# Low halves of split weights, kept in HBM and loaded again: one core of a hybrid recurrent decoder step

## The chip, the cores and the metric

One NeuronCore of a Trainium2 chip runs the kernel. It has five engines with instruction streams of their own, each in order: TensorE (PE; PEld is its weight load), VectorE (DVE), ScalarE (ACT), GpSimd (POOL) and SyncE (SP), which here issues every DMA. The metric is device time in microseconds (us) of one execution; the kernel before takes 3067.66 us (median of 3 runs, 3066.21 to 3068.48).

## The reference, cut to what matters

One layer of a decoder, for a prompt of 2048 tokens and 8 samples of 4 tokens, with 1024 channels, in fp32:

```python
h = layernorm(x)                                   # input layer norm, over 1024 channels
u = h @ w_in                                       # 1024 x 3860, columns for four groups of heads
y_a, y_b, y_c, y_d = delta(u_a), ssd(u_b), hgrn2(u_c), mlstm(u_d)   # chunkwise recurrences
mix = concat(y_a, y_b, y_c, y_d) @ w_out           # 1024 x 1024
h1 = layernorm(alpha * h + mix)
ff = square(relu(h1 @ w_up)) @ w_down              # 1024 x 4096, 4096 x 1024
out = layernorm(alpha * h1 + ff)
```

Outputs are `out` for prompt and samples, and the final states of the four recurrences.

## The kernel before, in words

The 2048 tokens are four blocks of 512 (`NB`, `TB`); the 32 sample tokens ride along with block 0 in the input projection and with block 2 afterwards, so those products are 544 wide. The order of stages is: input projection P of blocks 0 to 3, the output projection W of block 0 near the end of P 3, then for each block its feed-forward F, with W of the next block at F's end. The recurrences ("mixing", `gen_A` to `gen_D`) run in between, as chains of small operations on all engines, through P and most of F 0 to F 2.

**Products.** Weights come in *units* of 128 x 512 fp32 (256 KB): four 128x128 pieces of one column block. A product in fp32 accuracy is made of three passes in fp32r: a weight `w` is split into `hi = round(w)` and `lo = w - hi`, the data likewise, and PE adds `hi*xh + lo*xh + hi*xl`. In `gemm` each unit gives 12 matmuls (24 where the block is 544 wide). The list `units` (from `fill_units`) names all 832 units in order of use: 62 of w_in for each of four blocks, 16 of w_out for each, 64 of w_up for each, and 64 of w_dn for each, with the last 8 of them used twice in the last block.

**Supply of weights.** At each unit `cur`, `gemm` calls `w_pump`: it has SP load the raw units up to `cur + 4` (`w_get`, tile `wraw`), and splits the units up to `cur + 2` (`w_split`). A split is one operation that rounds (`whi`, on ACT mostly, line 253 like all operations of engines) and one subtraction (`wlo`, on POOL mostly, else on DVE). `wraw`, `whi` and `wlo` have four buffers each. A raw buffer comes free when its subtraction is done. Every block splits the same weights again. The first four units go another way, in `ln0_start`: `w_first` rounds, `w_rest` subtracts.

**What sets the order.** The program is written out by hand into one instruction stream for each engine while a planner (`_Run`) keeps an estimated clock for each engine. Each `tick` in `gemm` lets the mixing chains and the other streams go on that are ready by these clocks. `tvp` and `cpv` choose POOL or DVE, and ACT or DVE, by the same clocks. On the chip each engine follows its stream and waits on semaphores where its estimate was wrong. SP issues all DMAs in program order on one queue (line 374, `dma`); if one of them has to wait for its buffer or its data, those behind it wait too. The program gives SP's DMAs eight completion semaphores in turn, so a DMA also waits for the one eight places ahead of it.

**Input layer norm.** `ln0(b + 1)` runs beside P of block b: it normalizes, transposes, then stores the eight tiles of the block to `hTd` in HBM, which W reads again later, and splits six of them (`EARLY_P`).

Of the kernel before, what the change touches and what calls it, by code (L numbers as in the profile page):

```python
# [10 lines left out]
F32 = mybir.dt.float32  # L11
F32R = mybir.dt.float32r
# [10 lines left out]
TB = 512  # L23
# [15 lines left out]
EARLY_P = 6  # L39
# [4 lines left out]
LATE_W = 5.0  # L44
LATE_U = 3.0
LN1_PACE = 0.1
W0_AT = 29

# [297 lines left out]
def kernel(ctx: ExitStack, tc: tile.TileContext, t):  # L346
# [8 lines left out]
    sb4 = ctx.enter_context(tc.tile_pool(name="sb4", bufs=4))  # L355
    nbp = ctx.enter_context(tc.tile_pool(name="nbp", bufs=NBUF))
# [29 lines left out]
    def cp(out, in_, scale=1.0):  # L386
        A(out, in_, AF.Copy if scale == 1.0 else AF.Identity, scale)

    def tt(out, a, b, op, eng=None):
        (eng or V).tensor_tensor(out=out, in0=a, in1=b, op=op)  # L390
# [135 lines left out]

    def w_get(i):
        w = sb4.tile([128, 4, 128], F32, tag="wraw", name="wraw")
        dma(w, units[i])
        raws[i] = w  # L530

    def w_pump():
        cur = wst["cur"]
        while wst["nload"] < min(cur + 5, len(units)):
            i = wst["nload"]
            w_get(i)
            wst["nload"] += 1
            if wst["nsplit"] < min(cur + 3, wst["nload"]):
                w_split()
        while wst["nsplit"] < min(cur + 3, len(units)):  # L540
            w_split()

    def w_split():
        i = wst["nsplit"]
        w = raws.pop(i)
        hi = sb4.tile([128, 4, 128], F32R, tag="whi", name="whi")
        lo = sb4.tile([128, 4, 128], F32R, tag="wlo", name="wlo")
        cpv(hi, w, 512, LATE_W - 1.0)
        tt(lo, w, hi.bitcast(F32), sub, tvp(512, LATE_W))
        his[i] = (hi, lo)  # L550
        wst["nsplit"] += 1

    def w_first(i):
        hi = sb4.tile([128, 4, 128], F32R, tag="whi", name="whi")
        lo = sb4.tile([128, 4, 128], F32R, tag="wlo", name="wlo")
        cp(hi, raws[i])
        his[i] = (hi, lo)

    def w_rest(i, eng):
        hi, lo = his[i]  # L560
        tt(lo, raws.pop(i), hi.bitcast(F32), sub, eng)
# [109 lines left out]
    def ln0_start():  # L671
# [15 lines left out]
        w_get(3)  # L687
# [20 lines left out]
        w_rest(2, V)  # L708
        xs = xs[1:] + xs[:1]
# [20 lines left out]
        for k in range(8):  # L730
# [17 lines left out]
            if k == 5:  # L748
                for i in range(4, 8):
                    w_get(i)  # L750
                wst["nload"] = 8
# [12 lines left out]
    def ln0(b):  # L764
# [30 lines left out]
        yield from _stagger([one(i) for i in range(CPB)], 5)  # L795
        for k in range(8):
            dma(hTd[b][:, k, :], hT[b][k][:, 0:TB])
        queue_set(("P", b), hT[b], TB)
        for k in range(EARLY_P):
            yield  # L800
            split_next(("P", b))
# [1217 lines left out]
    def fill_units():  # L2019
        W = lambda: [units.extend([t["w_out_u"][d, 0], t["w_out_u"][d, 1]]) for d in range(8)]  # L2020
        for b in range(NB):
            for u in range(NPU):
                if b == NB - 1 and u == W0_AT:
                    W()
                units.extend([t["w_in_u"][u, 0], t["w_in_u"][u, 1]])
        for b in range(NB):
            f = 0
            for c in range(FFB):
                for j in range((4 if c == 0 else 3) + (1 if c + 1 < FFB else 0)):
                    units.extend([t["w_up_u"][f, 0], t["w_up_u"][f, 1]])  # L2030
                    f += 1
                if c == FFB - 1 and b + 1 < NB:
                    W()
                for q in range(2 if b == NB - 1 and c == FFB - 1 else 1):
                    units.extend(t["w_dn_u"][c, d] for d in range(8))
# [130 lines left out]
```

## Time and profile before

| | |
|---|---|
| median of 3 runs | 3067.66 us |
| the profiled execution, its time | 3071.5 us |
| its span, first to last instruction | 3069.7 us |
| PE busy | 2897.1 us, 94% |
| DVE, POOL, ACT busy | 2156.1, 1632.5, 1244.2 us |
| mean granted clock of PE | 0.983 |
| DMA | 407.10 MB, 133 GB/s; SP's queue takes 46.3% of the 16 DMA engines |

How to read it. Rows of groups give the line, engine and operation, then the tile written and the tiles read, the shape, how often, and behind the bar busy time in us and mean ns of one; behind the second bar the time in which the engine stood idle just before, and for whom. The tiles: `pd`, `pa`, `pb` are PSUM; `wraw`, `whi`, `wlo` the weights; `g` the 544-wide tiles of everything that isn't weights; `a`, `b`, `la..`, `kz..` those of the mixing chains; `U..`, `hTd`, `yTd` lie in HBM; `nb` is a tile broadcast from HBM (`ud32d`). Rows of waits give what an engine was about to run, for whom it waited, then the sum in us, the count and the longest. A matmul's end is modelled, so 100% busy says that PE had work, not that it ran at its peak.

### The profile page before, as it was taken

The page shows a single profiled execution, that of the slowest core. Times are in us where ns is not written, and L with a number is a line of the kernel's source. Part 1 is how long each engine was busy: PE and PEld are TensorE (multiplying, and loading weights), DVE is VectorE, ACT ScalarE, POOL GpSimd, SP SyncE. Part 2 cuts the span into 40 slices and gives each one's busy share as a digit, 9 for nine tenths or more (in the row PEclk, how much of TensorE's full clock was granted, in tenths as well). Part 3 has the DMA queues.
Part 4 walks back from the last instruction along what each step waited for, and adds up shares of the span by engine and source line. Part 5 has one row for each costly group of instructions (what it writes and reads, how often), then busy time and mean ns, then how long its engine had stood idle before and what let it go on. Part 6 is the DMA issues. An engine that isn't in the chain of part 4 may idle for free. (4 is left out here: it accounts for less than half of the span.)

```text
span 3069.7 us, 48033 instructions
## 1 busy us (share of the span) xinstructions
PE 2897.1 (94%) x16668; PEld 2479.8 (81%) x16668; DVE 2156.1 (70%) x4077; ACT 1244.2 (41%) x2653; POOL 1632.5 (53%) x1982
## 2 busy tenths in 40 slices
PE   7889899998999899999999999999999999999997
PEld 7778767777877778888787877778899999888886
DVE  6867887896986677777767865665887644474445
ACT  4554564564563533333244322233533222432222
POOL 5656664865664544554564536444363344444545
PEclk9999999999999999999999999999999999999998
DMA  6765465446556444454443435355343432333333
GB/s 188 85 186 166 121 190 164 130 129 201 121 159 192 139 120 124 132 173 119 138 145 115 144 91 139 118 159 153 92 147 105 125 93 84 112 120 93 99 95 98
DMA packets 361262, 407.10 MB, mean 133 GB/s; under 512 B 65468, under 2 KB 207804, under 8 KB 361020
## 3 DMA queue, kind: packets, MB, share of 16 engines
q1 hardware_dynamic: 361020, 404.04, 46.3%
q8 instruction: 132, 2.16, 0.3%
q14 instruction: 110, 0.90, 0.1%
HBM read 340.20 MB, written 63.72 MB: 132 GB/s over the span
## 5 line engine op out<-in xcount | busy, mean ns | idle before, releaser
L253 PE MATMUL pd<-g,whi 128*128 128x512 f32 (+2 forms) x8080 | 2242.6, 362 | 29.1 <-ACT g L253 17.2
L253 POOL TENSOR_TENSOR wlo<-wraw,whi 128x512 fp32r<-128x512 f32 x727 | 1031.8, 1426 | 1268.2 <-ACT whi L253 1071.8
L253 PEld LDWEIGHTS pd<-g,whi 128*128 128x128 f32 x8080 | 1393.6, 190 | 238.5 <-ACT g L253 19.4
L253 PE MATMUL pd<-g,wlo 128*128 128x512 f32 (+2 forms) x4040 | 1307.7, 355 | 16.4 <-POOL wlo L253 15.1
L253 PEld LDWEIGHTS pd<-g,wlo 128*128 128x128 f32 x4040 | 720.7, 190 | 113.2 <-POOL wlo L253 22.7
L253 ACT ACTIVATE whi<-wraw 128x512 fp32r<-128x512 f32 x797 | 489.2, 626 | 476.7 <-PE pd L253 256.0
L253 DVE TENSOR_TENSOR g<-g 128x512 fp32r<-128x512 f32 (+5 forms) x344 | 341.5, 995 | 157.2 <-ACT g L253 151.3
L253 ACT ACTIVATE g<-pd 128x512 f32<-128x512 f32 (+2 forms) x340 | 172.5, 526 | 473.7 <-PE pd L253 473.3
L253 DVE TENSOR_TENSOR g<-g,pd 128x512 f32<-128x512 f32 (+2 forms) x288 | 159.4, 570 | 211.7 <-PE pd L253 211.3
L253 ACT ACTIVATE g<-g 128x512 f32<-128x512 f32 (+4 forms) x350 | 212.9, 632 | 81.1 <-DVE g L253 40.1
L253 POOL TENSOR_TENSOR a<-nb,x 128x124 f32<-128x124 f32 (+30 forms) x496 | 198.4, 400 | 70.4 <-DMA nb<-ud32d 41.2
L253 POOL TENSOR_TENSOR x<-x,a 128x124 f32<-128x124 f32 (+30 forms) x496 | 199.5, 402 | 38.9
L253 DVE CAST g<-g 128x512 fp32r<-128x512 f32 (+1 forms) x162 | 158.4, 978 | 27.6 <-POOL g L253 21.2
L253 ACT ACTIVATE b<-b 128x256 f32<-128x256 f32 (+3 forms) x201 | 81.6, 406 | 182.2 <-DVE b L253 176.1
L253 DVE TENSOR_TENSOR wlo<-wraw,whi 128x512 fp32r<-128x512 f32 x105 | 83.1, 792 | 74.2 <-ACT whi L253 70.6
L253 DVE SCALAR_TENSOR_TENSOR g<-g 128x512 f32<-128x512 f32 (+3 forms) x124 | 117.8, 957 | 14.6 <-ACT g L253 14.2
L253 DVE SCALAR_TENSOR_TENSOR g<-g,par 128x512 f32<-128x512 f32 (+1 forms) x128 | 125.5, 998 | 0.1
L253 POOL TENSOR_TENSOR g<-g 128x512 f32<-128x512 f32 (+3 forms) x74 | 106.8, 1447 | 32.5 <-ACT g L253 25.1
L253 DVE TENSOR_TENSOR b<-laC 128x64 f32<-128x64 f32 (+3 forms) x466 | 110.2, 294 | 0.1
L253 DVE TENSOR_SCALAR g<-g 128x512 int32<-128x512 int32 (+6 forms) x137 | 79.7, 600 | 29.6 <-ACT g L253 28.7
L253 DVE TENSOR_TENSOR kzD<-laC,b 64x128 f32<-64x128 f32 (+1 forms) x228 | 98.6, 432 | 1.7
L253 DVE SCALAR_TENSOR_TENSOR g<-g,pd 128x512 f32<-128x512 f32 (+1 forms) x80 | 45.2, 581 | 67.0 <-PE pd L253 66.4
(2558 smaller groups left out, 2815.3 us busy)
## 6 DMA issues: line engine op xcount, KB each, us to landing
wraw<-in_w_dn_u_dram SPq DMA_DIRECT2D x264, 256.0 KB
wraw<-in_w_up_u_dram SPq DMA_DIRECT2D x256, 256.0 KB
wraw<-in_w_in_u_dram SPq DMA_DIRECT2D x248, 256.0 KB
nb<-ud32d SPq DMA_DIRECT2D x128, 256.0 KB
wraw<-in_w_out_u_dram SPq DMA_DIRECT2D x64, 256.0 KB
UC<-g SPq DMA_DIRECT2D x40, 256.0 KB
g<-in_x_prompt_dram SPq DMA_DIRECT2D x32, 256.0 KB
hTd<-g SPq DMA_DIRECT2D x32, 256.0 KB
```

The source lines that it names most:

```text
L253: r = f(*a, **k)
```

## The change

For each unit the program now counts its uses by name (`need`). A low half is subtracted at its first use, stored to HBM (`lod`) and from then on loaded beside the raw unit (`w_get`), straight into its buffer. For w_in the second making is the one stored (`KEEP`), so blocks 0 and 1 subtract and blocks 2 and 3 load. The store of unit i is issued when `cur` reaches i (`lo_keep`). `wraw` goes from four buffers to three, `wlo` from four to five. Of 832 low halves 268 are made, 206 stored and 564 loaded. In `ln0_start` the fourth unit is loaded after the first subtractions, and three units instead of four are loaded during the first transposes. In `ln0` the eight stores to `hTd` are issued one at each step of the stream, between the splits, and not in one go before them.

```diff
+KEEP = {"w_in_u": 2}
...
+    wrp = ctx.enter_context(tc.tile_pool(name="wrp", bufs=3))
+    wlp = ctx.enter_context(tc.tile_pool(name="wlp", bufs=5))
...
     def w_get(i):
-        w = sb4.tile([128, 4, 128], F32, tag="wraw", name="wraw")
+        w = wrp.tile([128, 4, 128], F32, tag="wraw", name="wraw")
         dma(w, units[i])
-        raws[i] = w
+        lo = None
+        if keys[i] in lod:
+            lo = wlp.tile([128, 4, 128], F32R, tag="wlo", name="wlo")
+            dma(lo.bitcast(F32), lod[keys[i]])
+        raws[i] = (w, lo)
+
+    def lo_make(i, hi, eng):
+
+        w, lo = raws.pop(i)
+        if lo is not None:
+            return lo
+        lo = wlp.tile([128, 4, 128], F32R, tag="wlo", name="wlo")
+        tt(lo, w, hi.bitcast(F32), sub, eng())
+        key = keys[i]
+        made[key] = made.get(key, 0) + 1
+        if made[key] == KEEP.get(key[0], 1) and uses[key] > made[key]:
+            kept.append((i, key, lo))
+        return lo
+
+    def lo_keep(n):
+        while kept and kept[0][0] <= n:
+            _, key, lo = kept.popleft()
+            lod[key] = drp.tile([128, 4, 128], F32, name=f"lod{len(lod)}")
+            dma(lod[key], lo.bitcast(F32))
 
     def w_pump():
         cur = wst["cur"]
+        lo_keep(cur)
         while wst["nload"] < min(cur + 5, len(units)):
...
     def w_split():
         i = wst["nsplit"]
-        w = raws.pop(i)
         hi = sb4.tile([128, 4, 128], F32R, tag="whi", name="whi")
-        lo = sb4.tile([128, 4, 128], F32R, tag="wlo", name="wlo")
-        cpv(hi, w, 512, LATE_W - 1.0)
-        tt(lo, w, hi.bitcast(F32), sub, tvp(512, LATE_W))
-        his[i] = (hi, lo)
+        cpv(hi, raws[i][0], 512, LATE_W - 1.0)
+        his[i] = (hi, lo_make(i, hi, lambda: tvp(512, LATE_W)))
         wst["nsplit"] += 1
...
         w_get(1)
-        w_get(3)
...
         w_rest(0, G)
         w_rest(2, V)
+        w_get(3)
...
             if k == 5:
-                for i in range(4, 8):
+                for i in range(4, 7):
                     w_get(i)
-                wst["nload"] = 8
+                wst["nload"] = 7
...
         yield from _stagger([one(i) for i in range(CPB)], 5)
+        queue_set(("P", b), hT[b], TB)
         for k in range(8):
             dma(hTd[b][:, k, :], hT[b][k][:, 0:TB])
-        queue_set(("P", b), hT[b], TB)
-        for k in range(EARLY_P):
-            yield
-            split_next(("P", b))
+            yield
+            if k < EARLY_P:
+                split_next(("P", b))
```

How the change moves instructions, at three places. First SP in P of block 2, around the stores of group A's gates (`UA`). In brackets stands what a DMA waits for: a compute engine, or one of the eight completion semaphores of earlier DMAs (`DMAHW`). Before:

```order
L374 DMA UA_169<-g 128x4x128 [waits DVE_49]
L374 DMA wraw<-in_w_in_u_dram 128x512 [waits DMAHW6_49,Pool_49]
L374 DMA wraw<-in_w_in_u_dram 128x512 [waits DMAHW7_49,Pool_49]
L374 DMA UA_169<-g 128x4x128 [waits DVE_49]
L374 DMA wraw<-in_w_in_u_dram 128x512 [waits DMAHW2_49,DMAHW0_49,Pool_49]
L374 DMA UA_169<-g 128x4x128 [waits DMAHW1_49,Pool_49]
```

After the change, at the same stores:

```order
L377 DMA UA_175<-g 128x4x128 [waits DVE_49]
L377 DMA UA_175<-g 128x4x128 [waits DMAHW0_49,DVE_49]
L377 DMA wraw<-in_w_in_u_dram 128x512 [waits DMAHW1_49,Activation_49]
L377 DMA wlo<-lod_4911 128x512 [waits DMAHW2_49,PE_49]
L377 DMA UA_175<-g 128x4x128 [waits DMAHW3_49,Pool_49]
L377 DMA UA_175<-g 128x4x128 [waits DMAHW4_49,DVE_49]
L377 DMA wraw<-in_w_in_u_dram 128x512 [waits DMAHW5_49,Activation_49]
L377 DMA wlo<-lod_4934 128x512 [waits DMAHW6_49,PE_49]
```

A raw load waited for POOL's subtraction; now it waits for the rounding on ACT, and a second load behind it waits for PE, whose matmuls free the `wlo` buffer.

Second, POOL at the first convolution of group A in P of block 2 (`a`, `x` are the scan of HGRN2, `halo` the convolution's border). Before:

```order
L253 TENSOR_TENSOR wlo<-wraw,whi 128x512
L253 COPY g<-haloA_119 128x3
L253 TENSOR_TENSOR wlo<-wraw,whi 128x512
L253 TENSOR_TENSOR a_5852<-nb,x_108 128x4x11
L253 TENSOR_TENSOR x_108<-x_108,a_5852 128x4x11
L253 TENSOR_TENSOR a_5852<-nb,x_108 128x4x10
```

After the change:

```order
L254 COPY g<-haloA_125 128x3
L254 TENSOR_TENSOR a_5984<-nb,x_114 128x4x11
L254 TENSOR_TENSOR x_114<-x_114,a_5984 128x4x11
L254 TENSOR_TENSOR a_5984<-nb,x_114 128x4x10
L254 TENSOR_TENSOR x_114<-x_114,a_5984 128x4x10
```

The subtractions are gone from POOL here. Over the whole program POOL's go from 727 to 224 and DVE's from 105 to 44; 20 operations of the last layer norm go from DVE to POOL.

Third, SP in P of block 1, at the input layer norm's stores of block 2. Before:

```order
L374 DMA wraw<-in_w_in_u_dram 128x512 x2
L374 DMA nb<-ud32d 128x1x512
L374 DMA hTd_152<-g 128x512 x8
L374 DMA wraw<-in_w_in_u_dram 128x512
L374 DMA UB_166<-g 128x4x128 x2
```

After the change:

```order
L377 DMA nb<-ud32d 128x1x512
L377 DMA hTd_158<-g 128x512
L377 DMA lod_5192<-wlo 128x512
L377 DMA wraw<-in_w_in_u_dram 128x512
L377 DMA UB_172<-g 128x4x128
L377 DMA lod_5229<-wlo 128x512
L377 DMA wraw<-in_w_in_u_dram 128x512
L377 DMA UB_172<-g 128x4x128
L377 DMA hTd_158<-g 128x512
```

The eight stores to `hTd` no longer stand in one row; between them stand the raw loads and, in this block, the stores of low halves.

More of the change, by code (lines that the diff above doesn't have):

```diff
@@ L525, with need @@
     raws, his = {}, {}
+    keys, uses, made, lod, kept = [], {}, {}, {}, deque()
+    def need(key, ap):
+        keys.append(key)
+        uses[key] = uses.get(key, 0) + 1
+        units.append(ap)
     def w_get(i):
-        w = sb4.tile([128, 4, 128], F32, tag="wraw", name="wraw")
+        w = wrp.tile([128, 4, 128], F32, tag="wraw", name="wraw")
         dma(w, units[i])
-        raws[i] = w
+        lo = None
[19 more added lines that the diff above has]
+            dma(lod[key], lo.bitcast(F32))
     def w_pump():
         cur = wst["cur"]
+        lo_keep(cur)
         while wst["nload"] < min(cur + 5, len(units)):
-            i = wst["nload"]
-            w_get(i)
+            w_get(wst["nload"])
             wst["nload"] += 1
@@ L554, in w_first @@
         hi = sb4.tile([128, 4, 128], F32R, tag="whi", name="whi")
-        lo = sb4.tile([128, 4, 128], F32R, tag="wlo", name="wlo")
-        cp(hi, raws[i])
-        his[i] = (hi, lo)
+        cp(hi, raws[i][0])
+        his[i] = (hi, None)
     def w_rest(i, eng):
-        hi, lo = his[i]
-        tt(lo, raws.pop(i), hi.bitcast(F32), sub, eng)
+        hi, _ = his[i]
+        his[i] = (hi, lo_make(i, hi, lambda: eng))
     def pieces(nt):
@@ L2019, in fill_units, with half @@
     def fill_units():
-        W = lambda: [units.extend([t["w_out_u"][d, 0], t["w_out_u"][d, 1]]) for d in range(8)]
+        def half(name, u):
+            for k in range(2):
+                need((name, u, k), t[name][u, k])
+        W = lambda: [half("w_out_u", d) for d in range(8)]
         for b in range(NB):
@@ L2024, in fill_units @@
                     W()
-                units.extend([t["w_in_u"][u, 0], t["w_in_u"][u, 1]])
+                half("w_in_u", u)
         for b in range(NB):
@@ L2029, in fill_units @@
                 for j in range((4 if c == 0 else 3) + (1 if c + 1 < FFB else 0)):
-                    units.extend([t["w_up_u"][f, 0], t["w_up_u"][f, 1]])
+                    half("w_up_u", f)
                     f += 1
@@ L2034, in fill_units @@
                 for q in range(2 if b == NB - 1 and c == FFB - 1 else 1):
-                    units.extend(t["w_dn_u"][c, d] for d in range(8))
+                    for d in range(8):
+                        need(("w_dn_u", c, d), t["w_dn_u"][c, d])
     fill_units()
```

## The prediction, made before the change was timed

> **What bounds the kernel now.** I read the page's busy line first, then the busy time of each engine by stage, then what PE and SP wait for.
>
> The page's first lines:
> ```profile
> span 3069.7 us, 48033 instructions
> PE 2897.1 (94%) x16668; PEld 2479.8 (81%) x16668; DVE 2156.1 (70%) x4077; ACT 1244.2 (41%) x2653; POOL 1632.5 (53%) x1982
> ```
> PE is the bound. The change removes no matmul, so it can pay only through the 173 us in which PE stands idle and through the granted clock. Where those lie, by stage (length, busy us of each engine, clock, DMA share, GB/s). The rows are: start; input projection of token blocks 0, 1, 2 and 3 (P0 to P3); feed-forward of blocks 0 and 1 (F0, F1); block 2 while mixing still runs (F2a) and after it; F3; the end:
> ```profile
> core 0: us, PE busy (x) PEld busy (x) DVE busy (x) ACT busy (x) POOL busy (x), PEclk, DMA share, GB/s
> 0.00:14.00 14.00, 0.63 (x2) 0.29 (x2) 9.13 (x22) 4.30 (x9) 6.13 (x32) 1.00 0.82 286
> 14.00:266.00 252.00, 221.53 (x1647) 215.76 (x1647) 187.26 (x338) 135.18 (x302) 153.13 (x152) 0.97 0.67 151
> 266.00:513.00 247.00, 227.72 (x1123) 182.06 (x1122) 202.68 (x374) 138.88 (x293) 142.78 (x171) 0.97 0.52 154
> 513.00:750.00 237.00, 216.01 (x1008) 170.70 (x1007) 195.21 (x336) 128.74 (x263) 156.03 (x177) 0.97 0.53 157
> 750.00:1045.00 295.00, 279.24 (x1397) 226.80 (x1396) 232.12 (x432) 156.36 (x326) 176.15 (x237) 0.98 0.56 156
> 1045.00:1618.00 573.00, 546.84 (x2862) 450.33 (x2861) 424.18 (x907) 214.47 (x485) 299.14 (x469) 0.98 0.45 134
> 1618.00:2188.00 570.00, 550.34 (x3177) 455.30 (x3175) 393.74 (x848) 194.10 (x433) 282.85 (x393) 0.99 0.43 127
> 2188.00:2423.00 235.00, 226.32 (x1821) 223.01 (x1821) 186.93 (x394) 83.50 (x211) 101.44 (x121) 1.00 0.41 122
> 2423.00:2685.00 262.00, 262.00 (x1938) 253.46 (x1936) 119.52 (x177) 80.35 (x149) 121.30 (x91) 1.00 0.36 104
> 2685.00:3015.00 330.00, 330.00 (x1452) 268.49 (x1452) 173.30 (x190) 91.64 (x159) 163.49 (x120) 1.00 0.35 101
> 3015.00:3070.00 55.00, 36.48 (x255) 33.64 (x253) 32.00 (x67) 16.69 (x30) 30.08 (x23) 0.85 0.34 104
> ```
> Length less PE busy is the idle time: 13.4 at the start, then P0 30.5, P1 19.3, P2 21.0, P3 15.8, F0 26.2, F1 19.7, F2a 8.7, then nothing for 592 us, and 18.5 at the end. So from 2423 to 3015 us nothing can be gained: POOL is as busy with low halves there as anywhere, and PE waits for none of it. As a share of the stage, idle falls with DVE's load: P2 8.9% at DVE 82%, P3 5.3% at 79%, F0 4.6% at 74%, F1 3.4% at 69%.
>
> What PE waited for in P2 and P3 (waited for: us, times, longest):
> ```profile
> PE pd L253 <- POOL wlo L253: 7.1, 8, 1.9
> PE pb__8189 L253 <- DVE b L253: 3.0, 1, 3.0
> PE pd L253 <- ACT whi L253: 1.9, 2, 1.0
> ```
> The low halves themselves are named for 7.1 of 36.8 us. The rest is many single waits of the mixing chains, mostly on DVE.
>
> **The change part by part.** The work that goes, and what POOL's work does to DVE (two shapes of one DVE operation, the second reading PSUM):
> ```profile
> L253 POOL TENSOR_TENSOR wlo<-wraw,whi 128x512 fp32r<-128x512 f32 x727 | 1031.8, 1426 | 1268.2 <-ACT whi L253 1071.8 <-PE pd L253 49.6 <-issue 42.3
> L253 DVE TENSOR_TENSOR wlo<-wraw,whi 128x512 fp32r<-128x512 f32 x105 | 83.1, 792 | 74.2 <-ACT whi L253 70.6 <-ACT dnD L253 2.3 <-POOL x L253 1.0
> L253 DVE TENSOR_TENSOR g<-g 128x512 fp32r<-128x512 f32 x156 | 166.9, 1073 | 21.2 <-ACT g L253 17.0
> L253 DVE TENSOR_TENSOR g<-g,pd 128x512 f32<-128x512 f32 x160 | 109.1, 682 | 134.6 <-PE pd L253 134.3
> ```
> Of 832 low halves 268 are still made (224 on POOL, 44 on DVE in the new order): all of blocks 0 and 1 of w_in, and the first use of w_out, w_up and w_dn. So 503 go from POOL, 503 x 1.426 = 717 us, and 61 from DVE, 61 x 0.792 = 48 us. Nearly all of that time is not PE's; what counts is where PE waits.
>
> *P2 and P3 (532 us, idle 36.8).* No low half of w_in is made here any more. DVE's largest groups in these two stages:
> ```profile
> L253 DVE SCALAR_TENSOR_TENSOR g<-g,par 128x512 f32<-128x512 f32 x64 | 64.6, 1035 | 0.1
> L253 DVE SCALAR_TENSOR_TENSOR g<-g 128x512 f32<-128x512 f32 (+1 forms) x61 | 57.1, 943 | 4.6 <-ACT g L253 4.4
> L253 DVE TENSOR_TENSOR wlo<-wraw,whi 128x512 fp32r<-128x512 f32 x28 | 23.5, 841 | 21.3 <-ACT whi L253 21.3
> L253 POOL TENSOR_TENSOR wlo<-wraw,whi 128x512 fp32r<-128x512 f32 x113 | 175.1, 1553 | 174.0 <-ACT whi L253 124.9 <-PE pd L253 19.1 <-DVE whi L253 12.9
> ```
> Against 682 ns, the first two groups lose 64 x 0.353 + 61 x 0.261 = 38.5 us beside POOL. The low halves are 175.1 of POOL's 332.2 us, 53%, so 20 us of that goes; with the 23.5 us of the third row DVE falls from 427 to some 384 us, from 80% to 72%. Between F0 and F1 (74% and 69%) that stands for 4% idle: 21.3 us, a gain of 15.5. Bounds: 7.1 (the named waits alone) and 36.8.
>
> *F1 and F2a (805 us, idle 28.4).* POOL is freed, but DVE makes few low halves here. I take half of the eight points by which DVE falls in P2 and P3; at the slope from F0 to F1 (1.2% of idle for 5 points) that is 1.0% of 805 us, a gain of 8. Bounds: 2 and 14 (half the idle).
>
> *The clock.* By the clock column P2, P3 and F1 lose 237 x 0.03 + 295 x 0.02 + 570 x 0.01 = 18.7 us, and the stage without idle has 1.00. Taken in proportion to the idle that goes, 13.0 x 15.5/36.8 + 5.7 x 8/28.4 = 7. Bounds: 0 and 18.7. The Trainium skill (TensorE: Matmul & The Clock Gate, HAM oscillation — how this bites in real kernels) states that gaps longer than about 3.4 us are what drops the clock. The trace of P2 doesn't agree, at 0.97 with no listed wait above 3.0 us; by that rule this term would be 0, and the sum 14.5 instead of 21.5.
>
> *What is added: 564 loads and 206 stores of 256 KB.* All go through SP's one queue. One unit is 0.262 MB; in F3, 101 GB/s takes a DMA share of 0.35, so 0.0035 for each GB/s. P2 gets 62 loads (69 GB/s, +0.24, to 0.77), P3 78 (to 0.80), P1 62 stores (to 0.75), F0 128 stores and 16 loads (to 0.68), F1 144 loads (to 0.66), F3 128 (to 0.70). None is full, and the first row of the stages shows 286 GB/s. But transfers will wait longer. What ACT already loses to that in P2 and P3, and SP over the whole run:
> ```profile
> L253 ACT ACTIVATE whi<-wraw 128x512 fp32r<-128x512 f32 x126 | 77.9, 624 | 33.4 <-DMA wraw<-in_w_in_u_dram 24.2 <-PE pd L253 4.7 <-POOL a L253 1.5
> SPq L374 <- POOL wlo L253: 918.7, 389, 10.6
> SPq L374 <- DMA nb<-ud32d: 45.9, 25, 3.9
> ```
> With share/(1 - share) as the measure of queueing, 0.55 to 0.78 is a factor of 2.9: ACT's 24.2 us become 70. PE saw 1.9 of 24.2 (the row of ACT whi above), 8%; of 46 more that is 4. With 1 for the mixing chains' broadcasts (nb) I take +5, from 0 to +46. For F1, at a lower share, +1.
>
> The second load of a unit waits for PE to finish the unit five back, since there are five buffers, and what stands behind it on SP waits too: the stores of U, the loads of the mixing chains, the next raw half. Now SP stands at the same place for POOL's low half (918.7 us in 389 waits) while PE runs on; so I price this at nothing beyond the +5. If the cover goes, it is the third rival below.
>
> *P1 and F0* keep making low halves, with stores, and with three raw buffers instead of four: a raw load now waits for the low half of the unit three back, one unit later than before. I take +3; 0 to +11 (P1 at P0's 12.1% idle: 247 x 0.121 - 19.3).
>
> *The start.* The fourth raw load waits for the first low half, which POOL made at:
> ```profile
> 15.08 1.25 POOL L253 TENSOR_TENSOR wlo<-wraw,whi 128x512 fp32r<-128x512 f32 x1
> 18.95 0.33 SPq L374 DMA_DIRECT2D hTx<-g  x1
> 22.75 0.61 ACT L253 ACTIVATE whi<-wraw 128x512 fp32r<-128x512 f32 x1
> ```
> So SP is held until 16.3 us, before its next issue at 18.95; and ACT rounds raw unit 1 at 22.75 and unit 3 only after that: 0, at most +4.
>
> *The end.* The last 16 units come as 512 KB in place of 256 KB. Four are there beforehand; the other 12, 6.3 MB, take 22 us at 286 GB/s, less than PE's 36.5 us in the last row of the stages. 0, at most +5.
>
> *Stores one by one.* The eight stores of one block held SP like this:
> ```profile
> 722.97 6.14 SPq L374 DMA_DIRECT2D hTd<-g  x8
> ```
> Three times some 6 us on SP, off PE's path; what PE loses is at most one wait of 3.0 us each (pb__8189, soon after). Taken at 0; down to -9.
>
> The sum: -15.5 - 8 - 7 + 5 + 1 + 3 = **-21.5 us**. The profiled execution took 3071.5 us (span and 1.8 around it), 3.8 above the median; 3071.5 - 21.5 = 3050.0, and from the median 3067.7 - 21.5 = **3046 us**.
>
> **The rivals.** *(1) The relief reaches further:* half of the idle time and of the clock's loss in P2, P3, F1 and F2a goes, (65.2 + 18.7)/2 = 42: 3026 us. For it: the steep fall of idle from 82% to 74% of DVE. Against: only 7.1 us name the low halves.
>
> *(2) The waits only move.* The order is laid out from estimated durations, and a chain that gets its operands earlier is placed earlier and is late by as much. PE's idle stays: 3066, give or take 6. For it: P3 has 3.6 points less idle than P2 at nearly the same DVE load.
>
> *(3) SP's queue decides; slower.* Each unit's second load stands at the head of SP until PE is through, with transfers that take longer. P0 is the stage with the largest DMA share, 0.67, and PE's idle share there is 12.1%. From that share on, I give P2 and P3 (0.77, 0.80) P0's rate: 532 x 0.121 - 36.8 = +27.6, with nothing gained in F1: 3095 us. Against: P0 also waits for scattered loads of the conv state, which the other blocks don't have.
>
> *(4) The clock is not given back,* because what idle time goes is in short waits and the few long ones remain: 14.5 us gained, 3053 us. The page on the clock gate named above would have it so.
>
> **How the numbers follow.** Forecast 0.36, rival 1 0.14, rival 2 0.16, rival 3 0.22, rival 4 0.12. Differences within 0.2%, 6 us, can hardly be told from none here. Faster: forecast, 1 and 4 nearly whole and a little of 2, 0.62; slower: 3 and a little of 2, 0.26; the same 0.12. The forecast's own range is 3032 to 3058. For 8 in 10 it must take in most of rival 1 and the lower part of rival 3: 3020 to 3086.
>
> **What would show it.** POOL's busy near 940 us; in P2 and P3 DVE near 72% and PE idle near 21 us in sum; DMA share 0.75 to 0.8 there; the span of F3 unchanged. Wrong it would be if PE's waits in P2 and P3 name DMA, or whi that waits for wraw, for more than 10 us; if P1 or F0 grow by more than 5 us; or if idle time stays while POOL's load halves.

## The result, and the profile after

The change made the kernel slower: 3087.3 us (median of 4 runs, 3079.3 to 3094.4) against 3067.2 us (4 runs), a ratio of 1.0052 with a 95% interval of 1.0033 to 1.0071, or +16 us (the medians differ by 20). The forecast was 3046 us, and the result lies just above the range of 3020 to 3086. The profiled execution of the changed kernel took 3079.3 us, the fastest of its runs and 7.8 us longer than the profiled one of before, so the profile shows less than half of the loss.

The first lines of the page after:

```profile
span 3077.5 us, 48291 instructions
PE 2894.4 (94%) x16668; PEld 2487.9 (81%) x16668; DVE 1800.7 (59%) x4007; ACT 1255.4 (41%) x2665; POOL 912.6 (30%) x1486
```

POOL lost 720 us of work, close to the 717 of the subtractions that go. DVE lost 355, of which only some 50 are subtractions (83.1 us before, 32.3 after); most of the rest are operations that became shorter. PE is busy for as long as before. The groups that shrank, and the DVE operation that was slowed beside POOL (1073 ns before):

```profile
L254 POOL TENSOR_TENSOR wlo<-wraw,whi 128x512 fp32r<-128x512 f32 x224 | 320.5, 1435 | 456.0 <-ACT whi L254 328.7 <-DMA wraw<-in_w_out_u_dram 31.6 <-DVE whi L254 24.2
L254 DVE TENSOR_TENSOR g<-g 128x512 fp32r<-128x512 f32 x155 | 118.6, 767 | 24.7 <-ACT g L254 20.3
```

By stage (same columns as before; P0, P1, P2, P3 with W of block 0, F0, F1, F2a, and the part of F3 in which nothing is waited for):

```profile
core 0: us, PE busy (x) PEld busy (x) DVE busy (x) ACT busy (x) POOL busy (x), PEclk, DMA share, GB/s
14.00:277.00 263.00, 228.48 (x1651) 220.80 (x1652) 186.75 (x345) 137.97 (x305) 151.15 (x150) 0.93 0.63 145
277.00:513.00 236.00, 222.41 (x1122) 180.20 (x1121) 189.79 (x367) 138.20 (x293) 146.26 (x171) 0.99 0.76 232
513.00:744.00 231.00, 214.84 (x1048) 175.13 (x1048) 156.22 (x381) 131.80 (x277) 68.38 (x141) 0.98 0.77 236
744.00:1049.00 305.00, 287.34 (x1454) 234.75 (x1453) 196.18 (x455) 160.25 (x331) 101.78 (x200) 0.98 0.74 222
1049.00:1639.00 590.00, 551.62 (x2901) 454.66 (x2900) 406.44 (x874) 215.98 (x491) 263.67 (x426) 0.98 0.63 196
1639.00:2221.00 582.00, 552.52 (x3162) 460.46 (x3161) 312.28 (x834) 195.12 (x438) 115.17 (x292) 0.97 0.66 193
2221.00:2400.00 179.00, 174.93 (x1423) 173.23 (x1422) 113.89 (x301) 71.76 (x168) 33.55 (x58) 1.00 0.63 195
2697.00:3025.00 328.00, 328.00 (x1438) 266.08 (x1437) 109.88 (x175) 95.08 (x165) 14.61 (x10) 1.00 0.63 194
```

Length less PE busy again gives idle time. P1 went from 19.3 to 13.6 us, P2 from 21.0 to 16.2, P3 with W from 21.2 to 17.7 (before, 750 to 1055 us). F0 went from 20.7 (1055 to 1619 us) to 38.4, and F1 from 20.5 (1619 to 2190 us) to 29.5. P0 grew by 11 us, of which 4 are idle time and 7 PE's busy time, at a clock of 0.93 instead of 0.97. From the start of F2 to the end it is the other way round: 856 us instead of 880. F3 by itself is untouched: 0.228 us a matmul, 0.227 before.

PE's longest single waits after the start, and what ACT waits for before it can round a raw unit (170 us in sum before, 337 now):

```profile
PE pa__23152 L254 <- DVE a L254: 7.3, 1, 7.3
PE pb__21413 L254 <- ACT whi L254: 6.4, 1, 6.4
PE pa__21947 L254 <- DVE a L254: 6.0, 1, 6.0
...
ACT whi L254 <- DMA wraw<-in_w_in_u_dram: 105.8, 48, 14.1
ACT whi L254 <- DMA wraw<-in_w_dn_u_dram: 89.4, 49, 10.5
ACT whi L254 <- DMA wraw<-in_w_up_u_dram: 87.1, 39, 7.1
```

The first of these waits can be followed back in the chain of waits (start, length, what) of that stretch of F1:

```profile
2114.23 8.98 DMA wraw<-in_w_out_u_dram
2123.22 0.02 issue
2123.24 0.02 SPq L377
...
2123.28 8.54 DMA wlo<-lod
2131.83 0.02 issue
2131.84 0.02 SPq L377
...
2131.89 10.89 DMA nb<-ud32d
...
2142.91 0.22 POOL a L254
...
2144.61 0.69 DVE a L254
2145.30 0.04 issue
2145.34 1.11 PE pa__23152 L254 x4
```

Three transfers of 256 KB make up 28 us of this chain. They are not neighbours: SP issues seven other DMAs between one and the next. Each of them is the DMA eight places ahead, whose completion semaphore the next one needs, and in this stretch loaded low halves take two or three of every eight places. The last of the three is the broadcast that a mixing chain needs. PE waits for DVE by name, but what was late is SP's queue with the loaded low halves in it.

Two rows mislead. SP's wait for POOL's low half (918.7 us before) became, for the larger part, a wait for PE, and POOL now stands long for the broadcast `nb`:

```profile
SPq L377 <- PE pd L254: 764.6, 431, 8.0
POOL a L254 <- DMA nb<-ud32d: 429.7, 76, 56.4
```

The second was 41.2 us before, which looks like ten times the lateness. A run below that adds no transfer at all shows 345.7 us in the same row: POOL merely has nothing else to do.

### The profile page after: what moved, and what is told of

It is laid out like the page before. It is cut to its first block, busy times and chain, and to the rows that moved or that the text cites. A ratio compares the mean times of both kernels' runs of the same rounds, so it can differ in the third digit from the quotient of the medians.

```text
span 3077.5 us, 48291 instructions
## 1 busy us (share of the span) xinstructions
PE 2894.4 (94%) x16668; PEld 2487.9 (81%) x16668; DVE 1800.7 (59%) x4007; ACT 1255.4 (41%) x2665; POOL 912.6 (30%) x1486
## 4 chain that ended last, share of the span: by engine, by line
PE 45%; DMA 11%; DVE 4%; POOL 3%; issue 2%; ACT 1%; SPq 1%; POOLq 0%; DVEq 0%; ACTq 0%
PE pd L254 38%; DMA nb<-ud32d 6%; DVE g L254 2%; DMA wraw<-in_w_out_u_dram 1%; POOL a L254 1%; DMA wraw<-in_w_dn_u_dram 1%; POOL x L254 1%; DMA wraw<-in_w_up_u_dram 1%; DVE a L254 1%; POOL wlo L254 1%; DVE b L254 1%; SPq L377 1%; ACT g L254 0%; DMA lod<-wlo 0%; DMA wlo<-lod 0%
## 5 line engine op out<-in xcount | busy, mean ns | idle before, releaser
L254 POOL TENSOR_TENSOR wlo<-wraw,whi 128x512 fp32r<-128x512 f32 x224 | 320.5, 1435 | 456.0 <-ACT whi L254 328.7
L254 DVE TENSOR_TENSOR g<-g 128x512 fp32r<-128x512 f32 (+5 forms) x343 | 260.4, 762 | 282.7 <-ACT g L254 271.9
L254 POOL TENSOR_TENSOR a<-nb,x 128x124 f32<-128x124 f32 (+30 forms) x496 | 180.8, 365 | 524.3 <-DMA nb<-ud32d 429.7
L254 ACT ACTIVATE g<-g 128x512 f32<-128x512 f32 (+3 forms) x355 | 215.8, 631 | 46.3 <-DVE g L254 37.7
L254 POOL TENSOR_TENSOR g<-g,lng 128x512 f32<-128x512 f32 x15 | 22.0, 1468 | 356.3 <-ACT g L254 356.3
L254 DVE SCALAR_TENSOR_TENSOR g<-g,par 128x512 f32<-128x512 f32 (+1 forms) x128 | 111.0, 883 | 5.0 <-ACT g L254 4.9
L254 DVE TENSOR_TENSOR b<-laC 128x64 f32<-128x64 f32 (+2 forms) x471 | 98.2, 267 | 11.3 <-DMA laC<-UC 11.3
L254 DVE SCALAR_TENSOR_TENSOR g<-g 128x512 f32<-128x512 f32 (+3 forms) x124 | 98.5, 797 | 10.2 <-ACT g L254 9.8
L254 DVE CAST g<-g 128x512 fp32r<-128x512 f32 (+1 forms) x157 | 87.8, 560 | 24.8 <-POOL g L254 18.1
L254 DVE TENSOR_TENSOR kzD<-laC,b 64x128 f32<-64x128 f32 (+1 forms) x228 | 83.1, 365 | 8.7 <-ACT b L254 7.0
```

The source lines that it names most:

```text
L254: r = f(*a, **k)
```

## The experiments

All ratios are against the kernel before, run on the same chip, with 95% intervals; us are worked out as ratio less one times the median of before (3067 to 3075 us). Two ladders were built: one takes the change apart, the other adds its parts to the kernel before without letting the planner move an instruction.

### The change taken apart

**Nothing kept.** All low halves are subtracted; buffers, start and layer norm stay as in the change.

```diff
-KEEP = {"w_in_u": 2}
+KEEP = {}
-        if made[key] == KEEP.get(key[0], 1) and uses[key] > made[key]:
+        if made[key] == KEEP.get(key[0], 99) and uses[key] > made[key]:
```

> The change without any keeping: every low half is subtracted each time, none is stored or loaded. What stays is three raw buffers, five low-half buffers, the later load of the fourth unit at the start and the stores of the input layer norm one by one. If the added transfers cost the time (theory 1: they come in bursts that fill the DMA engines), P of blocks 1 to 3 loses its gain of 24 us, F of blocks 0 and 1 loses nothing, and only P of block 0 keeps its loss of some 12 us: 3070 to 3082 us. If the smaller raw buffering or the start costs the time (theory 2), F of block 0 also stays longer: 3090 us or more. If it is the order, packed closer because POOL has less to do (theory 3), the order is that of before again: 3065 to 3072 us.

Measured: 3107.9 us, 1.0115 [1.0098, 1.0132], +35 us, as theory 2 had it. So the loss isn't in keeping as a whole: without it the rest of the change is slower still.

**Kept, loaded, and subtracted all the same**, over the loaded tile.

```diff
         if lo is not None:
+            tt(lo, w, hi.bitcast(F32), sub, eng())
             return lo
```

> The change with all its loads and stores, but each loaded low half is subtracted again over the loaded one, so that POOL and DVE save nothing and the added traffic stays. Against the run without keeping this is the price of the traffic alone, against the changed kernel the worth of what POOL and DVE save. Theory 1 (bursts of transfers): 30 to 60 us above the run without keeping, with idle time of PE in F of blocks 0 and 1 and raw loads named by ACT. Theory 3 (the order): within 8 us of the run without keeping, since the order is nearly the same.

Measured: 3153.6 us, 1.0274 [1.0251, 1.0296]. Against the run before this one, the added transfers cost 1.6%, 49 us; against the change, the subtractions that it leaves out are worth 2.2%, 68 us. Both figures hold something of the test's own, since here a subtraction also waits for the loaded tile.

**Only w_in kept, and all but w_in kept.**

```diff
-        if made[key] == KEEP.get(key[0], 1) and uses[key] > made[key]:
+        if made[key] == KEEP.get(key[0], 99) and uses[key] > made[key]:   # only w_in
...
-KEEP = {"w_in_u": 2}
+KEEP = {"w_in_u": 99}                                                     # all but w_in
```

> Only the low halves of w_in are kept (62 stores in block 1, 124 loads in blocks 2 and 3); those of w_out, w_up and w_dn are subtracted each time. Theory 1: P of blocks 1 to 3 keeps its gain of about 24 us, F of blocks 0 and 1 costs what it did before, P of block 0 stays at its loss of 12: some 3050 to 3062 us. Theory 2 (three raw buffers): F of block 0 stays slower: 3075 us or more.

> Only the low halves of w_out, w_up and w_dn are kept; those of w_in are subtracted each time. Theory 1: the gain of P of blocks 1 to 3 is gone and the loss in F of blocks 0 and 1 remains, 25 to 40 us: 3095 to 3115 us. Theory 3 (the order, through less work on POOL): P as before, F loses the same, since POOL is freed there.

Measured: only w_in 3073.0 us, 1.0009 [0.9992, 1.0025]; all but w_in 3136.3 us, 1.0211 [1.0196, 1.0226]. Against nothing kept (1.0115), keeping w_in gains 1.1% and keeping the feed-forward and output weights loses 1.0%. So w_in, on which the forecast for P2 and P3 rests, gains, and the other weights, on which the one for F1 and F2a rests, lose on balance. These are whole runs, not stages, and they don't add up: 33 us gained and 29 lost make 4, while keeping both gains 0.63%, 19 us.

**Nothing kept, four raw buffers** (four and four, as in the kernel before).

```diff
-    wrp = ctx.enter_context(tc.tile_pool(name="wrp", bufs=3))
-    wlp = ctx.enter_context(tc.tile_pool(name="wlp", bufs=5))
+    wrp = ctx.enter_context(tc.tile_pool(name="wrp", bufs=4))
+    wlp = ctx.enter_context(tc.tile_pool(name="wlp", bufs=4))
```

> The run without keeping, with four raw and four low-half buffers as before the change. If the third raw buffer's loss is what costs 37 us there (theory 2a: a raw load waits for the subtraction of one unit later, so raw halves come later for ACT), this comes back to 3065 to 3078 us, and ACT's waits for raw loads with it. If it is the stores one by one or the start (theory 2b), it stays at 3100 or more.

Measured: 3095.6 us, 1.0081 [1.0055, 1.0107]. One raw buffer less costs 0.34%, 10 us, hardly clear of the two intervals; 25 us of the 35 remain with no keeping and no buffer changed.

**The layer norm's stores in a row**, as before, without and with keeping.

```diff
-        queue_set(("P", b), hT[b], TB)
         for k in range(8):
             dma(hTd[b][:, k, :], hT[b][k][:, 0:TB])
+        queue_set(("P", b), hT[b], TB)
+        for k in range(EARLY_P):
             yield
-            if k < EARLY_P:
-                split_next(("P", b))
+            split_next(("P", b))
```

> The run without keeping, with the eight stores of the input layer norm in one row before the splits, as before the change. Theory 2a (raw buffers): within 8 us of the run without keeping, 3100 to 3116. Theory 2b (the stores and splits one by one): 3070 to 3085.

> The change with one part undone: the eight stores of the input layer norm are issued in a row before the splits, as before. By the prediction (that part taken at 0) it equals the change, 3087 within 6 us. If the stores one by one cost the change what they cost the kernel before by themselves (23 us), it is 15 to 25 us faster than the change, 3062 to 3072, about the same as before. If their cost is only that of another order, which falls either way, anything within 15 us of the change.

Measured: without keeping 3127.8 us, 1.0181 [1.0162, 1.0201]; with keeping 3133.2 us, 1.0189 [1.0175, 1.0204]. Both are slower than with the stores one by one, by 20 and by 42 us, and outside everything expected. And yet:

**Only the layer norm's stores one by one**, on the kernel before.

```diff
+        queue_set(("P", b), hT[b], TB)
         for k in range(8):
             dma(hTd[b][:, k, :], hT[b][k][:, 0:TB])
-        queue_set(("P", b), hT[b], TB)
-        for k in range(EARLY_P):
             yield
-            split_next(("P", b))
+            if k < EARLY_P:
+                split_next(("P", b))
```

> The kernel before with one edit of the change: the layer norm's stores one by one between the splits. Theory 4 (a new order costs): 3080 to 3105 us. Theory 2b (the edit itself is good or bad by SP's queue): 3060 to 3070, since SP no longer stands for 6 us at three places.

Measured: 3092.7 us, 1.0074 [1.0051, 1.0096], +23 us. The same edit costs 23 us here and saves 20 to 42 there. The planner charges each store an issue and a latency between two splits, so every later choice of the order moves. The edit thus changes SP's queue and the order at once, and no run changes one without the other. In the trace, with everything else as before, P3 with W of block 0 takes 323 us instead of 305, in many waits of mixing chains, none over 5.4 us; the two runs with nothing kept and the stores one by one show the same stage 20 and 17 us longer.

**A sham edit**, to see what another deal of the order costs by itself: the planner's estimate of a DMA's issue by 0.01 us.

```diff
-        R.cost("dma", 0.55, 2.5)
+        R.cost("dma", 0.56, 2.5)
```

> The kernel before with the planner's estimate for issuing a DMA at 0.56 us in place of 0.55: no operation, buffer or transfer is added or removed, only the order is dealt anew (a quarter of PE's rows stand elsewhere). Theory 4: 3080 to 3110 us. If the order doesn't matter: 3062 to 3076.

Measured: 3072.2 us, 1.0004 [0.9993, 1.0015]. In the trace another tile stands at about half of the places of PE's stream, and it costs nothing. So theory 4, by which any new order costs 10 us or more, doesn't hold.

### The parts at the order of before

In these kernels the planner is charged exactly what it was charged before (also for a subtraction that is left out, and not for the added transfers), so that the streams of PE and ACT are those of the kernel before row for row. They have four raw and four low buffers, low halves loaded three units ahead, and the start and the stores of before, unless told otherwise.

**Relief and traffic together, then for w_in alone.**

```diff
+        if lo is not None:
+            e = eng()
+            R.cost(e._name, e._cost("tensor_tensor", 512, None, {}), 0.15, True)
+            return lo
...
+    def lo_get(i):
...
+            nc.sync.dma_start(out=lo.bitcast(F32), in_=lod[keys[i]])
...
+        lo_keep(cur)
+        lo_get(cur + 3)
```

> Everything kept, four raw and four low-half buffers, low halves loaded three units ahead, but the planner is charged for each subtraction that is left out and not for the added transfers, and the start and the layer norm's stores are as before. So PE's and ACT's streams are those of before, row by row; DVE and POOL lack the subtractions, SP has the loads and stores besides. Theory 4 (every other variant was slow because the order was dealt anew by the planner's changed estimates, and any new order costs 10 to 40 us): without that the freed POOL and DVE give back idle time, 3035 to 3058 us. Theory 1 (the added transfers cost what POOL gives): 3060 to 3085.

> As the run in the order of before, but only w_in's low halves are kept. Theory 4: P of blocks 2 and 3 gains, 3045 to 3060 us, the rest as before. Theory 1: the same, since the feed-forward has no added transfers; so this one against the run with everything kept tells what the feed-forward's transfers cost or give at the same order.

Measured: 1.0003 [0.9986, 1.0021], +1 us, with all that the change keeps, 1.0019 [1.0002, 1.0036], +6 us, with w_in alone. At this order w_in alone gains nothing, unlike in the change's own. Either both sides are small, or they cancel. The next two runs take them one at a time.

**Relief alone.** Nothing is loaded or stored. In the 564 units concerned, `hi` is used where `lo` stood, so their low halves are left out of the products.

```diff
-            lo = wlp.tile([128, 4, 128], F32R, tag="wlo", name="wlo")
-            nc.sync.dma_start(out=lo.bitcast(F32), in_=lod[keys[i]])
+            lo = True
...
-            return lo
+            return hi
```

> The kernel before with its order of matmuls, its four raw buffers and its start; the subtraction of the 564 units that the change would load is left out and nothing is loaded or stored for it. In those units the second pass uses hi in place of lo, so the products lack the low halves of these weights (that part of the computation is left out). This measures the relief of POOL and DVE alone. By the sum of the prediction (15.5 + 8 + 7 us) it is 30 us faster than before, 3037. If the saved work is worth as much as the difference of the change and the run with traffic and subtraction says, 60 us or more is gained: under 3010. If waits only move, it is within 6 us of before.

Measured: 2984.0 us, 0.9701 [0.9686, 0.9716]: 92 us faster, three times the 30.5 of the prediction. P2, P3 with W of block 0, and F1 of this run:

```profile
508.00:714.00 206.00, 204.69 (x1008) 167.69 (x1007) 138.57 (x320) 126.30 (x262) 70.17 (x127) 1.00 0.58 174
...
714.00:1014.00 300.00, 282.55 (x1409) 230.64 (x1409) 192.60 (x436) 164.54 (x344) 106.02 (x206) 0.97 0.59 164
...
1570.00:2117.00 547.00, 542.78 (x3177) 452.18 (x3176) 307.54 (x822) 194.00 (x435) 113.42 (x276) 1.00 0.46 133
```

In P2 idle time falls from 21.0 to 1.3 us, and the same 1008 matmuls take 204.7 us in place of 216.0. The clock, 1.00 in place of 0.97, accounts for some 7 of these 11 us (237 x 0.03); the runs don't show what the rest is. In P3 little changes: idle time goes from 21.2 to 17.4 us and the clock from 0.98 to 0.97, though DVE is relieved there too. F2 after the mixing, where PE waits for nothing and all units use `hi` twice, takes 262 us as before, so the other data don't speed PE up. PE's longest waits in P2:

```profile
PE pa__7729 L254 <- ACT a L254: 0.8, 1, 0.8
PE pb__7818 L254 <- DVE b L254: 0.4, 1, 0.4
PE pb__6181 L254 <- DVE b L254: 0.2, 1, 0.2
```

The largest group of DVE in P2, of the kernel before and of this run:

```profile
L253 DVE SCALAR_TENSOR_TENSOR g<-g,par 128x512 f32<-128x512 f32 x32 | 33.5, 1080 | 0.0
```

```profile
L254 DVE SCALAR_TENSOR_TENSOR g<-g,par 128x512 f32<-128x512 f32 x32 | 24.4, 797 | 3.0 <-ACT g L254 2.9
```

One operation became 283 ns shorter, and DVE now waits for its data where it never did. Over the whole run PE's listed waits for DVE fall from 72 to 26 us and those for POOL from 22 to 14, while ACT's waits for raw units only go from 170 to 151. So the relief reaches PE mostly through DVE's chains; raw units hardly come sooner. And POOL's wait for the broadcast over the whole run, the row promised above, with no transfer added:

```profile
POOL a L254 <- DMA nb<-ud32d: 345.7, 65, 41.0
```

**Traffic alone.** All loads and stores, and every subtraction still made, over the loaded tile.

```diff
-            R.cost(e._name, e._cost("tensor_tensor", 512, None, {}), 0.15, True)
+            tt(lo, w, hi.bitcast(F32), sub, e)
```

> The kernel before with its order on PE, ACT, POOL and DVE, its four raw buffers and its start; every load and store of the change is added, low halves loaded three units ahead, and the subtraction is still made over the loaded tile. This measures the traffic alone. By the prediction (+5, +1 and most of +3) it is 6 to 9 us slower than before, 3076. If the traffic costs about what the relief gives, so that the two cancel in the run with both at the same order, it is 30 to 60 us slower, 3098 to 3128. If traffic is harmless and buffers or order made the loss, it is within 6 us of before.

Measured: 3177.3 us, 1.0336 [1.0320, 1.0353]: 103 us slower. So the two do cancel: -2.99% and +3.36% make +0.37%, beside the 0.03% of the run with both. On top of the relief, with no subtraction behind them, the transfers cost 3.02%, 93 us (0.9701 to 1.0003); 10 of the 103 are thus the test's own or an interplay. P2 and F1 of this run:

```profile
514.00:773.00 259.00, 218.00 (x1010) 171.06 (x1009) 189.98 (x337) 130.28 (x266) 154.89 (x182) 0.95 0.69 209
...
1677.00:2288.00 611.00, 562.90 (x3176) 462.37 (x3174) 379.86 (x849) 196.78 (x436) 277.57 (x393) 0.97 0.61 181
```

PE's longest waits in P2:

```profile
PE pd L254 <- POOL wlo L254: 12.6, 9, 3.9
PE pb__6243 L254 <- DVE b L254: 10.3, 1, 10.3
PE pb__8384 L254 <- DVE b L254: 5.0, 1, 5.0
```

Idle time in P2 is twice that of before, and the largest single waits are again mixing chains on DVE; the low halves come to 12.6 us in nine waits.

**Is it the bytes, or SP's waits?** First the bytes without the waits: each load goes to a place in HBM that nothing reads. Then the waits without the bytes: same loads and stores, 16 of 512 columns.

```diff
-            nc.sync.dma_start(out=lo.bitcast(F32), in_=lod[keys[i]])
+            nc.sync.dma_start(out=aside[at[0]], in_=lod[keys[i]])              # bytes
...
-            nc.sync.dma_start(out=lo.bitcast(F32), in_=lod[keys[i]])
+            nc.sync.dma_start(out=lo[:, 0, 0:16].bitcast(F32), in_=lod[keys[i]])   # waits
```

> The run with the traffic alone (before's order and buffers, every subtraction still made), but each of the 564 loads goes to a place in HBM that nothing reads, so that it waits for no buffer and nothing waits for it; the stores stay. If the traffic costs by filling the DMA engines, so that raw weights and the mixing chains' transfers land later, most of the 100 us stays: 3140 us or more. If it costs because SP stands at the load until PE has given the buffer free and because the subtraction waits for the load, most of it goes: 3070 to 3100. The prediction had +6 to +9 for the traffic: 3077.

> The run with the traffic alone (before's order and buffers, every subtraction still made), with the same loads and stores at the same places in SP's queue and the same waits for buffers, but only 16 of the 512 columns are moved: 8 KB in place of 256 KB. If the traffic costs by filling the DMA engines, nearly all of the 100 us goes: 3070 to 3090. If it costs because SP stands at the load until PE has given the buffer free, most of it stays: 3140 or more. Between the two, the parts can be read off together with the run whose loads go aside.

Measured: bytes alone 3122.8 us, 1.0175 [1.0162, 1.0189], +54 us; waits alone 3113.1 us, 1.0142 [1.0126, 1.0158], +44 us. Both, in nearly equal parts, and together they make nearly the whole 103. Neither run is pure: both keep the 770 added places in a queue in which each DMA waits for the one eight ahead, and the loads put aside go from HBM to HBM. What those places cost by themselves wasn't tested. The rows of the second, in which SP stands for PE's buffers though hardly a byte is moved, and POOL for a tile that SP issued late:

```profile
SPq L548 <- PE pd L254: 1009.0, 462, 8.9
...
POOL wlo L254 <- DMA wlo<-lod: 291.6, 146, 14.9
```

The second row belongs to this test and not to the change, where nothing subtracts over the loaded tile; so 44 us is rather an upper value for SP's waits in the change.

**Three raw buffers and the change's start alone.**

```diff
-    wrp = ctx.enter_context(tc.tile_pool(name="wrp", bufs=4))
-    wlp = ctx.enter_context(tc.tile_pool(name="wlp", bufs=4))
+    wrp = ctx.enter_context(tc.tile_pool(name="wrp", bufs=3))
+    wlp = ctx.enter_context(tc.tile_pool(name="wlp", bufs=5))
```

> The kernel before with its order on all compute engines, nothing kept, nothing loaded besides; only three raw buffers and five for low halves in place of four and four, and the start with the fourth raw unit loaded after the first subtractions, as in the change. This measures the buffers and the start alone. By the prediction (+3, start 0) within 6 us of before. If the twelve us between three and four raw buffers without keeping are due to the buffers and not to another order, 10 to 15 us slower: 3080.

Measured: 3092.5 us, 1.0056 [1.0043, 1.0070], +17 us.

**Where each part falls.** Since these streams are those of before, the time between the starts of the same two matmuls can be compared stage by stage. Differences to before in us, from one profiled execution each:

| stage (before, us) | relief | traffic | both | bytes | waits | 3 raw buffers |
|---|---|---|---|---|---|---|
| P0 (251) | -6 | -2 | -2 | -3 | -4 | +5 |
| P1 (248) | 0 | +2 | 0 | +1 | -1 | 0 |
| P2 (237) | -31 | +22 | -12 | +6 | +11 | +4 |
| P3, W (304) | -4 | +17 | +10 | +9 | +6 | -2 |
| F0, W (565) | -10 | +18 | +16 | +20 | +3 | +5 |
| F1, W (571) | -23 | +41 | +5 | +13 | +21 | +8 |
| F2 to the end (880) | -13 | +7 | -10 | +1 | +4 | +2 |

F0 stores 128 low halves, gets little relief, and pays mostly in bytes. P2 and F1 have both large, P2 with a gain left over.

### Versions with four raw buffers

The change with four raw and four low buffers and low halves loaded three ahead; then the same with only w_in kept and the start as before.

```diff
-    wrp = ctx.enter_context(tc.tile_pool(name="wrp", bufs=3))
-    wlp = ctx.enter_context(tc.tile_pool(name="wlp", bufs=5))
+    wrp = ctx.enter_context(tc.tile_pool(name="wrp", bufs=4))
+    wlp = ctx.enter_context(tc.tile_pool(name="wlp", bufs=4))
...
         lo_keep(cur)
+        lo_get(cur + 3)
...
-        if made[key] == KEEP.get(key[0], 1) and uses[key] > made[key]:
+        if made[key] == KEEP.get(key[0], 99) and uses[key] > made[key]:   # second version
```

> The change with everything kept, but four raw and four low-half buffers, and each low half loaded three units ahead (with four buffers it can't be four). Theory 2a: the third buffer's 37 us come back, so 3087 less about 37: 3045 to 3060 us. If the added transfers (46 us with no saving) rule whatever the buffers, 3075 to 3095.

> Only w_in's low halves kept, four raw and four low-half buffers, loads three units ahead, and the start as before the change. Theory 2a and the gain of keeping w_in (33 us against the run without keeping): 3030 to 3050 us, faster than both kernels. If the buffers aren't the cause: 3070 to 3080.

Measured: all kept 3069.1 us, 0.9988 [0.9976, 1.0000]; only w_in kept 3063.4 us, 0.9978 [0.9966, 0.9990]. The second is faster than both kernels, by 7 us against before, though not by the 18 to 38 that were expected. The first shows where the loss of the change is: with all low halves kept, four raw buffers instead of three (and loads three ahead instead of four) take off 0.64%, 20 us, and nothing of the loss is left.

## Why the prediction was wrong

**P2 and P3, -15.5; F1 and F2a, -8: too small.** The step that failed is reading idle time from the line between F0 and F1, at 74% and 69% of DVE. With relief alone, DVE falls in P2 to 67% (138.6 of 206 us) and idle time not to 4% but to 0.6%. In P3 DVE falls from 78% to 64%, yet idle time stays at 5.8% (17.4 of 300 us). So idle time doesn't follow DVE's share from one stage to another; F0 and F1, which have other chains and, in F0, low halves of their own, were no yardstick. In F1, relief alone takes 15 of the 20 us of idle time. The mechanism, POOL's work slowing DVE and DVE the mixing chains, was right: 1080 ns became 797, and PE's waits for DVE fell by 46 us.

**The clock, -7: about right for the relief, of the other sign in the change.** By the clock column, as the prediction reckoned it, P2, P3 with W, and F1 lose 18.9 us before (237 x 0.03 + 305 x 0.02 + 571 x 0.01). With relief alone they lose 9.0 (300 x 0.03, all in P3), which is a gain of 10. In the change they lose 28.2 (231 x 0.02 + 305 x 0.02 + 582 x 0.03), which is 9 more than before: F1 now has waits of 6.0 to 7.3 us, and P0 loses 11 more besides. The lower clock in P2 and F1 before came with waits of 3.0 and 3.2 us at most, and it was full once these were gone. The rule that the prediction quoted from the Trainium skill (TensorE: Matmul & The Clock Gate, HAM oscillation — how this bites in real kernels), that gaps longer than about 3.4 us drop the clock, would have given nothing in these stages; the measurement decides against it, and with it against the reason given for rival 4.

**Added transfers, +5 and +1: the step that failed worst, and the one that turned the sign.** They cost 49 us in the change's own ladder and 93 to 103 at the order of before. The forecast of ACT's wait was good: 70 us for P2 and P3, and the trace has 65.6 there:

```profile
ACT whi L254 <- DMA wraw<-in_w_in_u_dram: 51.1, 22, 5.6
ACT whi L254 <- DMA wraw<-in_w_out_u_dram: 14.5, 4, 7.6
```

What failed is the 8%, PE's share of this by the waits that name `whi`. A late transfer can reach PE through the mixing chains, under the name of DVE, as the chain in F1 shows for the longest wait there. Over the whole run PE's listed waits for DVE are 72 us before, 26 with relief alone, 123 with traffic alone and 87 in the change. In P2 and P3 of the change PE's waits that name `whi` come to 2.3 us, so the sign of error that the prediction set on them, 10 us, never showed. And F1's +1 rested on its lower DMA share, where traffic cost 41 us at a share of 0.61: the mean share doesn't show how long a DMA waits for the one eight places ahead or for a buffer.

**SP's wait for PE, at nothing: failed.** That SP stood just as long for POOL before didn't make it free: with hardly a byte moved, the added loads and their waits cost 44 us, an upper value for this step.

**P1 and F0, +3; start 0.** Three raw buffers cost 10 us without keeping and 20 in the change, and together with the start 17 at the order of before, there mostly in P0, F0 and F1. P0 was left out of this step, though its low halves wait for the same buffers. P1 grew by 2 us at most at the order of before and became 12 us shorter in the change; F0 grew by 25, past the 5 us named as the mark of an error. At the order of before it is the added bytes that lengthen F0, by 20 us, and three raw buffers add 5.

**Stores one by one, 0: not a constant.** The edit costs 23 us alone and its undoing costs 42 in the change. It moves both SP's queue and the order; which of them counts isn't shown, but the waits of 6 us on SP, on which the step rested, don't give such figures.

**End and F3, 0: right.** F3 takes the same time per matmul, though its DMA share rose from 0.35 to 0.63.

**The rivals.** The sign was rival 3's, and its 3095 us is nearest: SP's queue and longer transfers do outweigh the gain. That is partly luck. Its place is wrong: P2 and P3 have less idle time than before, and the loss sits in P0, F0 and F1. And the relief that it left out of account is as large as its cost. Rival 1 (the relief reaches further) is right as a mechanism and larger than it said; it is paid back. Rival 2 (the waits only move) falls, since with relief alone the waits go.

**The sum, and what stays open.** In the change's ladder: stores one by one +23, the rest without keeping and with four raw buffers +2, three raw buffers +10, transfers +49, subtractions saved -68, which is the +16 measured; it closes because each term is the difference of two neighbouring runs. Keeping thus gains 19 net. The forecast for it was 24.5 (-15.5 - 8 - 7 + 5 + 1), close only by luck: the two terms are two and eight times as large as forecast. At the order of before, relief and transfers together were +1 (-92 and +103 by themselves), and three raw buffers with the start +17; that is +18, next to the +16 of the change. With the 20 us that four raw buffers take off the change, the likeliest account is that relief and transfers cancel and that the third raw buffer, priced at +3, is what is left as the loss. What the new order and the stores one by one add to this isn't settled: that edit was worth +23, -20 and -42 us in three places, and the sham edit 1.

## What to carry to other kernels

Work taken off a helper engine can be worth several times its named waits, and a transfer put in its place can cost as much: measure the two apart, at one fixed order of instructions, before netting them. A load that waits for a consumer's buffer holds up everything behind it on an in-order queue, and a mean DMA share well below one doesn't make it safe; a second queue for it would be the next thing to try, which no run here did. Before giving a buffer of the old stream to a new one, time that by itself. Which weights are worth keeping isn't settled: w_in alone gained 33 us in the change's own order and cost 6 at the order of before.

## What the hardware showed that was not expected

The granted clock responded to short gaps: in P2 it was 0.97 with no wait above 3.0 us and 1.00 with none above 0.8, worth some 7 us (237 x 0.03) of the 11.3 by which the same 1008 matmuls became shorter. And with eight DMAs of one queue under way, single transfers of 256 KB took 8.5 to 10.9 us from issue to landing, in a stage where the 16 DMA engines were busy two thirds of the time.
